# Scoring the HGRN2 levels in two column halves, with a score tile ordered by chunk half

## The chip, the cores and the metric

The kernel runs on one core of a Trainium2 chip. The metric is device time in microseconds for one execution of the whole layer (2048 tokens, width 1024, F32 inputs and outputs). Below, PE is TensorE's matmul unit and PEld its weight load, DVE is VectorE, ACT is ScalarE, POOL is GpSimd and SP is SyncE.

## The reference

The reference is one decoder layer: two head groups side by side (a gated linear recurrence, HGRN2, with 4 heads of width 128, and a sliding-window attention with sinks), an output projection, a gated MLP with a causal convolution, and a final norm. The change concerns the recurrence only. In each chunk of 64 tokens the reference computes, for each head,

```
b      = cumsum(log_f)                       # per key channel
scores = einsum('bhtk,bhsk,bhtsk->bhts', q, k, exp(b_t - b_s)),  s <= t
intra  = einsum('bhts,bhsv->bhtv', scores, v)
inter  = einsum('bhtk,bhkv->bhtv', q * exp(b), state)
out    = intra + inter
state  = state * exp(b_last) + einsum('bhsk,bhsv->bhkv', k * exp(b_last - b), v)
```

with k = 1 - f. The decay between a query t and a key s differs by channel, so the scores are not one plain matmul.

## The kernel before, in words

The sequence is worked in two halves of 1024 tokens (`for hf in range(NH)`, L1103). Each half has a mixing stage (recurrence and attention, 42 to 372 us and about 1100 to 1437 us of the span) and an MLP stage. In the mixing stage the generators `hgrn` (one for each head) and `attend` (one for each pair of query heads) are advanced in the order written out in ORDER (L40): `f`, `q`, `l`, `s` and `p` are the five steps of a recurrence head, `qa`, `sc`, `pv` and `pw` those of attention. Within that order a scheduler at build time interleaves the instructions of the steps on each engine; matmuls of a later step fill the places where an earlier one would wait. The large projections run as three matmuls in a reduced F32 form with 512 (L218) or 256 (L630 to L632) moving columns; the small matmuls of the recurrence and of the attention output (L446) run in full F32, which leaves two records for each matmul in the profile.

Step `l` computes the scores of all chunks. The kernel uses chunks of 128 tokens (TT = 8 of them in a half) and splits the decay by levels m = 1, 2, 4, ..., 64. At level m the tokens fall into blocks of 2m; keys of the first m and queries of the last m of a block meet, and their decay is the product of what each has gathered up to the border between them. K and Q are multiplied by these factors as the levels go on (L523 and L524, or L534 and L535). The tokens of the second four chunks of a half lie in reversed order within groups of 32, so "first" and "last" change places there.

The tile ST holds the scores of a head: partitions are keys, then chunk, then 128 queries.

- L481: GpSimd clears keys 64 to 127 against queries 0 to 63. L486 computes the diagonal, 64 keys by 64 queries in each matmul, 16 matmuls; L489 writes it to ST through the identity.
- Levels 1 to 16 (L512 to L524, L540 to L545): ScalarE gathers into G the keys of chunk u and of chunk u + 4 that are keys at this level (L515). One matmul for each of four u multiplies 128 such keys by 128 queries (64 of each chunk) into a PSUM tile of 512 columns (L517). Only blocks that belong together are wanted; VectorE copies them into ST under a mask (L542).
- Level 32 (32 columns of weights, 32 moving) and level 64 (64 columns of weights, 64 moving, in the two column halves of the array in turn): L531, copied to ST by ScalarE (L548, L552).

Step `s` transposes K (L564), forms the state updates (L571) and chains the states in SS (L575, L578). Step `p` adds, for each chunk, scores times values and queries times state into PSUM (L590, L592), squares the result on ScalarE for the norm (L593), scales it and transposes it. The eight chunks of a half take two PSUM tiles of four chunks each, `po`.

Of the kernel before, what the change touches and what calls it, by code (L numbers as in the profile page):

```python
# [8 lines left out]
F32 = mybir.dt.float32  # L9
# [3 lines left out]
AF = mybir.ActivationFunctionType  # L13
# [4 lines left out]
P = 128  # L18
# [5 lines left out]
TT = HALF // P  # L24
# [25 lines left out]
def hymba_layer(ctx: ExitStack, tc: tile.TileContext, a: dict, out: bass.AP, rows_out: bass.AP):  # L50
    nc = tc.nc
# [275 lines left out]
        v = t.rearrange("p (g r) -> p g r", r=32)  # L327
        return v[:, :, ::-1] if turn else v

    def across(t, base, dims):  # L330

        v = t[:, :]
        return bass.AP(v.tensor, v.offset + base, [list(v.ap[0])] + dims)

    def rows(kv):
        return slice(kv * HD, (kv + 1) * HD)
# [123 lines left out]
    def hgrn(hf, h, X, invb, vs, WG, gates, mix, p, fu=None):  # L460
# [16 lines left out]
        nc.vector.tensor_tensor(Q, q, f, op=ALU.mult)  # L477


        ST = p.tile([P, TT, P], F32, tag="t4", name="ST", bufs=2)  # L480
        nc.gpsimd.memset(ST[rows(1), :, 0:64], 0.0)  # L481
        pd = ps("hg", "pdiag")
        for c in range(TT):
            for k in range(2):
# [1 line left out]
                nc.tensor.matmul(pd[rows(k), c * 64:(c + 1) * 64], K[:, ts], q[:, ts], start=True, stop=True)  # L486
        for k in range(2):
            r = rows(k)
            nc.vector.tensor_tensor(ST[r, :, r], pd[r].rearrange("p (c t) -> p c t", t=64),  # L489
                                    ident[r, r].unsqueeze(1).to_broadcast([64, TT, 64]), op=ALU.mult)  # L490


# [15 lines left out]
        for m in LEVELS:  # L508
            nb = HALF // (2 * m)
            pl = ps("hg", "plev")  # L510
            if m < 32:
                n, nu = 64 // m, TT // 2  # L512
                far, near = [[512 - m, 2], [P, nu], [2 * m, n], [1, m]], [[512 + m, 2], [P, nu], [2 * m, n], [1, m]]
                G = p.tile([P, 512], F32, tag="G", name="G", bufs=2)
                nc.scalar.copy(across(G, 0, [[m, 2], [P, nu], [2 * m, n], [1, m]]), across(K, 0, near))  # L515
                for u in range(nu):
                    marks[m] = nc.tensor.matmul(across(pl, u * 64, [[256, 2], [1, 64]]), G[:, u * P:(u + 1) * P],  # L517
                                                across(Q, u * P + m, [far[0]] + far[2:]), start=True, stop=True)
                nf = P // m
                Kv, Qv = across(K, 0, near), across(Q, m, far)  # L520
                Fk = across(F, 1, [[4 * nf - 1, 2], [nf, nu], [2, n], [0, m]])
                Fq = across(F, 0, [[4 * nf + 1, 2], [nf, nu], [2, n], [0, m]])
                nc.vector.tensor_tensor(Kv, Kv, Fk, op=ALU.mult)  # L523
                nc.vector.tensor_tensor(Qv, Qv, Fq, op=ALU.mult)  # L524
            else:
                Qv = Q.rearrange("p (b w m) -> p b w m", w=2, m=m)
                Kv = K.rearrange("p (b w m) -> p b w m", w=2, m=m)
                for c in range(TT):
                    for s0 in range(0, P, 2 * m):
                        o = pl[s0:s0 + m, c * m:(c + 1) * m] if m < 64 else pl[rows(c % 2), c // 2 * m:(c // 2 + 1) * m]  # L530
                        nc.tensor.matmul(o, K[:, c * P + s0:c * P + s0 + m],  # L531
                                         Q[:, c * P + s0 + m:c * P + s0 + 2 * m], start=True, stop=True)
                Fv = F.rearrange("p (b w) -> p b w", w=2)
                nc.vector.tensor_tensor(Qv[:, :, 1], Qv[:, :, 1], Fv[:, :, 0:1].to_broadcast([P, nb, m]), op=ALU.mult)  # L534
                nc.vector.tensor_tensor(Kv[:, :, 0], Kv[:, :, 0], Fv[:, :, 1:2].to_broadcast([P, nb, m]), op=ALU.mult)  # L535
# [3 lines left out]
            F = Fn  # L539
            if m < 32:  # L540
                mk = C.lmask[m].bitcast(U32).rearrange("p s t -> p (s t)")
                nc.vector.copy_predicated(across(ST.rearrange("p c t -> p (c t)"), m, far),  # L542
                                          across(mk, 0, [[64, 2], [0, nu], [m, n], [1, m]]),
                                          pl.rearrange("p (s u b m) -> p s u b m", s=2, u=nu, m=m))
                continue  # L545
            if m == 64:
                for k in range(2):
                    nc.scalar.copy(ST[0:m].rearrange("p (c k) t -> p c k t", k=2)[:, :, k, m:],  # L548
                                   pl[rows(k), 0:TT // 2 * m].rearrange("p (c m) -> p c m", m=m))
                continue  # L550
            for s0 in range(0, P, 2 * m):
                nc.scalar.copy(ST[s0:s0 + m, :, s0 + m:s0 + 2 * m],  # L552
                               pl[s0:s0 + m, 0:TT * m].rearrange("p (c m) -> p c m", c=TT))
        yield
        v = vs[h]
# [26 lines left out]
        on = p.tile([P, TT, P], F32, tag="t4", name="on", bufs=2)  # L582
        ss = p.tile([P, TT], F32, tag="ss", name="ss", bufs=2)
        po = [ps("hg", "po") for _ in range(NB)]
        for c in range(TT):
            cs = slice(c * P, (c + 1) * P)
            prev = state[:, h] if c == 0 else SS[:, c - 1]
            o = po[c // 4][:, c % 4 * P:(c % 4 + 1) * P]
            empty = hf == 0 and c == 0
            marks["po"] = nc.tensor.matmul(o, ST[:, c], v[:, c], start=True, stop=empty)  # L590
            if not empty:
                marks["po"] = nc.tensor.matmul(o, Q[:, cs], prev, start=False, stop=True)  # L592
            nc.scalar.activation(on[:, c], o, AF.Square, accum_out=ss[:, c:c + 1])  # L593
        rs = rsqrt(ss, TT, 1.0 / P)
        if h == HG - 1:
            mix[h] = new_x()
# [605 lines left out]
```

## Time and profile before

| what | us |
|---|---|
| median of 3 runs | 2149.85 (2149.7 to 2150.18) |
| span of the profiled execution | 2149.0 |
| the profiled execution's own time beside it | not listed apart from the three runs; they lie 0.7 to 1.2 above the span |
| PE busy | 2130.8 |
| DVE busy | 1632.2 |
| ACT busy | 1020.2 |
| first mixing stage (42 to 372): PE, DVE, ACT busy | 328.6, 228.7, 163.0 |
| second mixing stage (1100 to 1437): PE, DVE, ACT busy | 335.6, 229.9, 165.3 |

A row of a timeline reads: start in us from the start of the span, time from the first start to the last end, engine, line, operation, output<-input, rows by columns of the weights, moving operand, how many of the same follow each other, and in brackets idle time of the engine before it with what ended it. Matmuls overlap, and the end of one is modelled; so the price of a group is read from start to start of what stands around it. A group of one line (in the views by line) gives minimum, median and maximum duration in ns, first and last start, and the shapes.

### The profile page before, as it was taken

The numbers are of one execution on the slowest core, as the hardware profiler recorded it, in microseconds if no ns is written. First come the engines' busy times: TensorE is split into PE (matmuls) and PEld (weight loads), VectorE is DVE, ScalarE is ACT, GpSimd is POOL, SyncE is SP. The second block draws the span as 40 slices with busy tenths as digits, with TensorE's granted clock in tenths as the row PEclk, the third lists the DMA queues.
The fourth block names the chain that finished last, engine by engine and source line by source line (L and its number), as shares of the span: only waits on it lengthen the run. The fifth ranks groups of instructions, "written<-read, shape, count | busy, mean of one in ns | idle before, by whom it ended". The sixth has DMA issues, their size and how long they took to land.

```text
span 2149.0 us, 29228 instructions
## 1 busy us (share of the span) xinstructions
PE 2130.8 (99%) x11271; PEld 1790.6 (83%) x11271; DVE 1632.2 (76%) x2443; ACT 1020.2 (47%) x1818; POOL 16.2 (1%) x45
## 2 busy tenths in 40 slices
PE   8999999999999999999999999999999999999998
PEld 6988988888888888888889889888888888888887
DVE  6576768788887888785775767677988888787765
ACT  5445554564444445345634446535544444443453
POOL 2000000000000000000000000000000000000000
PEclk9999999999999999999999999999999999999999
DMA  4111012413332334974641111124223323359743
GB/s 158 40 30 40 31 30 79 137 62 125 94 122 89 103 118 147 371 255 145 217 138 40 30 31 33 40 75 158 69 104 103 118 84 122 95 187 398 236 147 133
DMA packets 91147, 254.41 MB, mean 118 GB/s; under 512 B 11136, under 2 KB 13952, under 8 KB 91008
## 3 DMA queue, kind: packets, MB, share of 16 engines
q1 hardware_dynamic: 90576, 252.29, 35.3%
q8 instruction: 88, 1.44, 0.3%
q14 instruction: 51, 0.42, 0.1%
q10 hardware_dynamic: 432, 0.27, 0.0%
HBM read 195.37 MB, written 57.15 MB: 118 GB/s over the span
## 4 chain that ended last, share of the span: by engine, by line
PE 93%; DVE 5%; ACT 1%; issue 1%; DMA 0%; SPq 0%; DVEq 0%; ACTq 0%
PE X L767 7%; PE X L766 7%; PE X L765 7%; PE pop L218 6%; PE q L218 4%; PE f L218 4%; PE hq L218 4%; PE Y L767 4%; PE Y L765 4%; PE Y L766 4%; PE pdx L954 3%; PE pdx L953 3%; PE pdx L952 3%; PE g L218 3%; PE pdy L953 3%; PE pdy L954 3%
## 5 line engine op out<-in xcount | busy, mean ns | idle before, releaser
L638 ACT CAST whi<-raw 128x1024 fp32r<-128x1024 f32 x88 | 92.7, 1053 | 115.5 <-PE X L766 71.1
L765 PE MATMUL X<-T,whi 128*128 128x512 f32 x352 | 136.9, 389 | 0.0
L766 PE MATMUL X<-T,whi 128*128 128x512 f32 x352 | 136.9, 389 | 0.0
L767 PE MATMUL X<-T,wlo 128*128 128x512 f32 x352 | 136.9, 389 | 0.0
L836 DVE SCALAR_TENSOR_TENSOR y<-ga,cw,y 128x1024 f32<-128x1024 f32 x88 | 112.7, 1280 | 25.9 <-ACT y L834 25.8
L639 DVE TENSOR_TENSOR wlo<-raw,whi 128x1024 fp32r<-128x1024 f32 x88 | 107.3, 1219 | 4.4 <-ACT whi L638 4.4
L771 ACT COPY u<-X 128x512 f32<-128x512 f32 x88 | 51.6, 586 | 122.5 <-PE X L767 122.2
L199 ACT CAST whi<-raw 128x1024 fp32r<-128x1024 f32 x58 | 60.5, 1048 | 98.8 <-issue 20.6
L639 DVE TENSOR_TENSOR xld<-raw,xhd 128x1024 fp32r<-128x1024 f32 x72 | 81.1, 1132 | 17.8 <-ACT xhd L638 17.6
L638 ACT CAST xhd<-raw 128x1024 fp32r<-128x1024 f32 x72 | 69.8, 978 | 39.1 <-DMA raw<-act0T 14.0
L218 PE MATMUL pop<-XL,whi 128*128 128x512 f32 x256 | 84.2, 392 | 0.9 <-DVE XL L230 0.9
L218 PE MATMUL pop<-XH,wlo 128*128 128x512 f32 x256 | 83.3, 391 | 0.8 <-DVE wlo L200 0.8
L218 PE MATMUL pop<-XH,whi 128*128 128x512 f32 x256 | 83.1, 396 | 0.8 <-ACT XH L229 0.5
L200 DVE TENSOR_TENSOR wlo<-raw,whi 128x1024 fp32r<-128x1024 f32 x58 | 70.5, 1220 | 9.8 <-ACT whi L199 9.8
L767 PEld LDWEIGHTS X<-T,wlo 128*128 128x128 f32 x352 | 66.1, 188 | 13.7
L766 PEld LDWEIGHTS X<-T,whi 128*128 128x128 f32 x352 | 66.1, 188 | 13.7
L765 PEld LDWEIGHTS X<-T,whi 128*128 128x128 f32 x352 | 66.0, 188 | 13.7
L630 PE MATMUL pvv<-whi,XH 128*128 128x256 f32 x256 | 73.0, 286 | 0.0
L631 PE MATMUL pvv<-whi,XL 128*128 128x256 f32 x256 | 72.9, 286 | 0.0
L632 PE MATMUL pvv<-wlo,XH 128*128 128x256 f32 x256 | 71.9, 285 | 0.0
L767 PE MATMUL X<-B,wlo 128*128 128x512 f32 x176 | 68.7, 390 | 0.7 <-DVE wlo L639 0.7
L765 PE MATMUL X<-T,Sh 128*128 128x512 f32 x176 | 68.7, 390 | 0.0
(390 smaller groups left out, 6399.2 us busy)
## 6 DMA issues: line engine op xcount, KB each, us to landing
wr<-in_w_down SPq DMA_DIRECT2D x90, 512.0 KB, 5.6
raw<-in_w_gate SPq DMA_DIRECT2D x44, 512.0 KB, 3.6
raw<-in_w_up SPq DMA_DIRECT2D x44, 512.0 KB, 3.6
raw<-act0T SPq DMA_DIRECT2D x20, 512.0 KB, 5.9
raw<-act1T SPq DMA_DIRECT2D x20, 512.0 KB, 5.6
act0B<-y SPq DMA_DIRECT2D x33, 256.0 KB, 2.3
act1B<-y SPq DMA_DIRECT2D x33, 256.0 KB, 2.4
raw<-in_w_out SPq DMA_DIRECT2D x16, 512.0 KB, 3.7
```

The source lines that it names most:

```text
L218: nc.tensor.matmul(o[b], w, x[:, bs], start=f, stop=l)
L630: nc.tensor.matmul(o[:, 0:256], xh[:, t], hi[:, c], start=kt == 0, stop=False)
L631: nc.tensor.matmul(o[:, 0:256], xl[:, t], hi[:, c], start=False, stop=False)
L632: nc.tensor.matmul(o[:, 0:256], xh[:, t], lo[:, c], start=False, stop=kt == KT - 1)
L638: nc.scalar.copy(h, src)
L639: return (eng or nc.vector).tensor_tensor(l, src, h.bitcast(F32), op=ALU.subtract)
L765: nc.tensor.matmul(o, wh[:, ws], xh, start=i == 0 and not more, stop=False, skip_group_check=more)
L766: nc.tensor.matmul(o, wh[:, ws], xl, start=False, stop=False, skip_group_check=more)
L767: nc.tensor.matmul(o, wl[:, ws], xh, start=False, stop=i == 3, skip_group_check=more)
L836: nc.vector.scalar_tensor_tensor(y, g[:, w:w + HALF], C.cw[:, ft, w:w + 1], y, op0=ALU.mult, op1=ALU.add)
L953: nc.tensor.matmul(o, wh[:, i, c], al[:, i, cols], start=False, stop=False, skip_group_check=more)
L954: nc.tensor.matmul(o, wl[:, i, c], ah[:, i, cols], start=False, stop=l, skip_group_check=more)
```

## The change

The matmul of levels 1 to 16 becomes two, one for each half of a 128-column piece of G: 64 keys by the 64 queries that can belong to them. The half k writes PSUM partitions 64k to 64k + 63, so 256 columns of the PSUM tile are used in place of 512. The masked copy becomes two as well, one for each half of the partitions. ST is ordered by chunk half: partition, then half of the queries (64 each), then chunk, then query. The diagonal, the copies of levels 32 and 64 and the clearing follow the new order. In step `p` the matmul of scores and values becomes two, one for each half of a chunk's queries, which write the two halves of the PSUM partitions; for each PSUM tile all eight of them come first, then the four matmuls of queries and state, each followed by its square.

```
-    def across(t, base, dims):
+    def across(t, base, dims, r=slice(0, P)):
-        v = t[:, :]
+        v = t[r, :]
...
-        ST = p.tile([P, TT, P], F32, tag="t4", name="ST", bufs=2)
-        nc.gpsimd.memset(ST[rows(1), :, 0:64], 0.0)
+        ST = p.tile([P, 2, TT, 64], F32, tag="t4", name="ST", bufs=2)
+        nc.gpsimd.memset(ST[rows(1), 0], 0.0)
...
-            nc.vector.tensor_tensor(ST[r, :, r], pd[r].rearrange("p (c t) -> p c t", t=64),
+            nc.vector.tensor_tensor(ST[r, k], pd[r].rearrange("p (c t) -> p c t", t=64),
...
+                half = [[2 * m, n // 2], [1, m]]
                 for u in range(nu):
-                    marks[m] = nc.tensor.matmul(across(pl, u * 64, [[256, 2], [1, 64]]), G[:, u * P:(u + 1) * P],
-                                                across(Q, u * P + m, [far[0]] + far[2:]), start=True, stop=True)
+                    for k in range(2):
+                        t0 = u * P + k * 64
+                        marks[m] = nc.tensor.matmul(across(pl, u * 32, [[P, 2], [1, 32]], rows(k)), G[:, t0:t0 + 64],
+                                                    across(Q, t0 + m, [far[0]] + half), start=True, stop=True)
...
-                nc.vector.copy_predicated(across(ST.rearrange("p c t -> p (c t)"), m, far),
-                                          across(mk, 0, [[64, 2], [0, nu], [m, n], [1, m]]),
-                                          pl.rearrange("p (s u b m) -> p s u b m", s=2, u=nu, m=m))
+                for k in range(2):
+                    nc.vector.copy_predicated(
+                        across(ST.rearrange("p k c t -> p (k c t)"), k * 512 + m, [[256 - m, 2], [64, nu]] + half, rows(k)),
+                        across(mk, k * 32, [[64, 2], [0, nu], [m, n // 2], [1, m]], rows(k)),
+                        pl[rows(k), 0:256].rearrange("p (s u b m) -> p s u b m", s=2, u=nu, m=m))
...
-                    nc.scalar.copy(ST[0:m].rearrange("p (c k) t -> p c k t", k=2)[:, :, k, m:],
+                    nc.scalar.copy(ST[0:m, 1].rearrange("p (c k) t -> p c k t", k=2)[:, :, k],
...
-                nc.scalar.copy(ST[s0:s0 + m, :, s0 + m:s0 + 2 * m],
+                nc.scalar.copy(ST[s0:s0 + m, s0 // 64, :, m:],
...
-        for c in range(TT):
-            cs = slice(c * P, (c + 1) * P)
-            prev = state[:, h] if c == 0 else SS[:, c - 1]
-            o = po[c // 4][:, c % 4 * P:(c % 4 + 1) * P]
-            empty = hf == 0 and c == 0
-            marks["po"] = nc.tensor.matmul(o, ST[:, c], v[:, c], start=True, stop=empty)
-            if not empty:
-                marks["po"] = nc.tensor.matmul(o, Q[:, cs], prev, start=False, stop=True)
-            nc.scalar.activation(on[:, c], o, AF.Square, accum_out=ss[:, c:c + 1])
+        for b in range(NB):
+            at = [po[b][:, i * P:(i + 1) * P] for i in range(4)]
+            empty = hf == 0 and b == 0
+            for i in range(4):
+                for k in range(2):
+                    marks["po"] = nc.tensor.matmul(at[i][rows(k)], ST[:, k, 4 * b + i], v[:, 4 * b + i],
+                                                   start=i == 0, stop=empty and i == 0, skip_group_check=True)
+            for i in range(4):
+                c = 4 * b + i
+                if not (empty and i == 0):
+                    marks["po"] = nc.tensor.matmul(at[i], Q[:, c * P:(c + 1) * P], SS[:, c - 1] if c else state[:, h],
+                                                   start=False, stop=True, skip_group_check=True)
+                nc.scalar.activation(on[:, c], at[i], AF.Square, accum_out=ss[:, c:c + 1])
```

## The prediction

> **What bounds the kernel now.** I read the page first: shares of busy time, then the chain that ended last.
>
> ```profile
> span 2149.0 us, 29228 instructions
> ```
> ```profile
> PE 2130.8 (99%) x11271; PEld 1790.6 (83%) x11271; DVE 1632.2 (76%) x2443; ACT 1020.2 (47%) x1818; POOL 16.2 (1%) x45
> ```
> ```profile
> PE 93%; DVE 5%; ACT 1%; issue 1%; DMA 0%; SPq 0%; DVEq 0%; ACTq 0%
> ```
>
> TensorE is busy all the time and carries 93% of the chain. The span is 2149.0 us and the median of the runs 2149.85, so 0.85 us lie around the span; I keep that constant. The busy time of PE is no price list, since matmuls overlap: what counts is the distance from one start to the next. So I went to the timeline of PE and read prices there. The change touches only the two mixing stages; this is the first (start:end, its length, then busy us of PE, PEld, DVE, ACT, POOL), with its last 36 us in the second row:
>
> ```profile
> 42.00:372.00 330.00, 328.59 (x2367) 287.57 (x2366) 228.74 (x430) 163.02 (x429) 1.57 (x3) 1.00 0.14 42
> 336.00:372.00 36.00, 34.64 (x277) 28.70 (x276) 27.14 (x49) 13.04 (x46) 0.00 (x0) 1.00 0.22 73
> ```
>
> PE idles 1.4 us of 330 (330.00 - 328.59), nearly all of it in the last 36 (36.00 - 34.64). A microsecond of PE work that goes there is a microsecond of time, as long as nothing else steps in.
>
> **The levels.** An F32 matmul leaves two records:
>
> ```profile
> L517 PE MATMUL plev<-Q,G x320: 270/275/382, 62.3 to 1415.5; 128*128 128x128 f32 x160
> ```
>
> That is 160 matmuls: 2 halves of the sequence, 4 heads, 5 levels, 4 each; so 40 level groups of 8 records. The change makes each matmul two, on 64 keys and 64 queries: 16 records per group. Level 64 already has exactly that shape (64 columns of weights, 64 moving, the two column halves in turn), so the trace has the new price. First a group of before in the stream of 256-wide matmuls:
>
> ```profile
> 73.50 0.28 PE L631 MATMUL pvv<-whi,XL 128*128 128x256 f32 x1
> 73.62 1.06 PE L517 MATMUL plev<-Q,G 128*128 128x128 f32 x8
> 74.43 0.36 PE L632 MATMUL pvv<-wlo,XH 128*128 128x256 f32 x1
> 74.63 0.28 PE L630 MATMUL pvv<-whi,XH 128*128 128x256 f32 x1
> ```
>
> Then level 64 in the same stream:
>
> ```profile
> 91.61 0.28 PE L632 MATMUL pvv<-wlo,XH 128*128 128x256 f32 x1
> 91.81 0.69 PE L531 MATMUL plev<-Q,K 128*64 128x64 f32 x16
> 92.43 0.39 PE L630 MATMUL pvv<-whi,XH 128*128 128x256 f32 x1
> 92.65 0.28 PE L631 MATMUL pvv<-whi,XL 128*128 128x256 f32 x1
> 92.77 0.28 PE L632 MATMUL pvv<-wlo,XH 128*128 128x256 f32 x1
> ```
>
> A 256-wide matmul takes 0.12 us of the stream (92.65 to 92.77). The old group takes 74.63 - 73.50 - 2 x 0.12 = 0.89; the new shape 92.65 - 91.61 - 0.24 = 0.80. So a group that stands alone gains only 0.09 us. The 16 small records themselves are quick, but going from full-width weights to 64 columns costs 0.08 (0.20 instead of 0.12 before 91.81), and coming back costs a tail before 92.43 and 0.10 after it.
>
> A group that stands beside other 64-column work saves that passage. The first level of each head (8 groups) follows the diagonal scores, which are 64 x 64 already:
>
> ```profile
> 61.23 1.15 PE L486 MATMUL pdiag<-hg,K 128*64 128x64 f32 x32
> 62.31 1.18 PE L517 MATMUL plev<-Q,G 128*128 128x128 f32 x8
> 63.24 0.72 PE L218 MATMUL q<-XL,whi 128*128 128x512 f32 x2
> ```
>
> 32 records take 1.08 to the next start, 16 took 0.62 (91.81 to 92.43): 0.46 for 16 more. The old group took 62.31 to 63.24, 0.93. Gain 0.47 each.
>
> Six groups stand beside the 64-column matmuls of the attention output; the first and the last of them, each with its neighbour:
>
> ```profile
> 159.75 1.05 PE L517 MATMUL plev<-Q,G 128*128 128x128 f32 x8
> 160.74 0.44 PE L446 MATMUL poT<-pp,V 128*64 128x128 f32 x4
> ```
> ```profile
> 1414.40 0.31 PE L446 MATMUL poT<-po,V 128*64 128x128 f32 x2
> 1414.64 1.16 PE L517 MATMUL plev<-Q,G 128*128 128x128 f32 x8
> ```
>
> and level 64 between such matmuls:
>
> ```profile
> 269.63 0.64 PE L531 MATMUL plev<-Q,K 128*64 128x64 f32 x16
> 270.09 0.39 PE L446 MATMUL poT<-pp,V 128*64 128x128 f32 x4
> ```
>
> 0.99 becomes 0.46 to 0.54 plus 0.08 for going in: a gain of 0.37 to 0.45; I take 0.42, as one of the six has such a neighbour on both sides. Levels in all: 8 x 0.47 + 6 x 0.42 + 26 x 0.09 = **-8.6 us**.
>
> **The outputs.** The score tile is now stored by halves, so each chunk's scores times values becomes two matmuls with 64 columns of weights and 128 moving. This is where the change pays. The nearest shape is the attention output again, here a run of 8 such rows, its first, its last and what follows:
>
> ```profile
> 282.57 0.44 PE L446 MATMUL poT<-pp,V 128*64 128x128 f32 x4
> 282.84 0.39 PE L446 MATMUL poT<-po,V 128*64 128x128 f32 x4
> ...
> 283.93 0.39 PE L446 MATMUL poT<-pp,V 128*64 128x128 f32 x4
> 284.15 0.39 PE L446 MATMUL poT<-po,V 128*64 128x128 f32 x4
> 284.47 0.50 PE L218 MATMUL f<-XL,whi 128*128 128x512 f32 x1
> 284.80 0.62 PE L218 MATMUL f<-XH,wlo 128*128 128x512 f32 x2
> 285.26 0.62 PE L218 MATMUL f<-XH,whi 128*128 128x512 f32 x2
> ```
>
> and the old form:
>
> ```profile
> 115.40 0.39 PE L590 MATMUL po<-v,ST 128*128 128x128 f32 x2
> 115.62 0.28 PE L592 MATMUL po<-SS,Q 128*128 128x128 f32 x1
> ```
>
> Before, one chunk is 2 records, 0.22 us. After, it is 4 records, and 4 of them also take 0.22 (283.93 to 284.15). The halving gains nothing here, and the passage is new. The change groups four chunks, so 16 blocks: each pays 0.08 going in, 0.05 at its first row (282.57 to 282.84 is 0.27), 0.10 at its end (284.15 to 284.47 is 0.32) and 0.10 on the next matmul (0.33 to 284.80, against 0.46 for the two after it): 0.33. Four heads' outputs already follow attention outputs, the first and last of these:
>
> ```profile
> 208.59 0.39 PE L446 MATMUL poT<-po,V 128*64 128x128 f32 x4
> 208.91 0.71 PE L590 MATMUL po<-v,ST 128*128 128x128 f32 x4
> ```
> ```profile
> 1431.25 0.49 PE L590 MATMUL po<-v,ST 128*128 128x128 f32 x2
> ```
>
> There the passage is paid today (0.32 from 208.59 to 208.91) and only moves: 0. So 12 x 0.33 = **+4.0 us**; bounds 2.6 (one block per head, both banks together) and 5.3 (all 16 alone).
>
> **VectorE, ScalarE, GpSimd.** Each masked copy into the score tile becomes two, on 64 partitions and half the columns:
>
> ```profile
> L542 DVE COPY_PREDICATED ST<-lmask,plev x40: 693/726/1341, 65.2 to 1416.6; 128x512 f32<-128x512 uint32 x40
> ```
> ```profile
> L408 DVE COPY_PREDICATED sc<-own,psc x64: 391/443/508, 100.7 to 1403.9; 128x256 f32<-128x256 uint32 x64
> ```
>
> 2 x 0.44 against 0.73: 0.16 more, 40 times, some 6.5 us on an engine with 228.7 of 330 busy. It is hidden by PE's own work, which doesn't wait for the score tile until much later. The cover is gone where the last head's levels run out of other work:
>
> ```profile
> 349.51 0.68 PE L517 MATMUL plev<-Q,G 128*128 128x128 f32 x4 [0.44 <-DVE Q L524]
> ```
>
> Queued behind a masked copy there are the next level's K and Q products. Three copies at the end of each mixing stage, 0.16 each, twice: at most 0.9, and four of the six gains beside attention outputs (1.6 us) lie in these stretches and could turn into waiting. Bounds 0 and +2.5. I take **+0.3**, nearer to 0: the level's own matmuls also end 0.1 to 0.4 sooner, which hands the K and Q products back about what the copies take. The other score copies and GpSimd's memset move as many elements as before and stay off PE's path; no DMA is added or moved, and no new wait stands on any queue.
>
> **Sum.** -8.6 + 4.0 + 0.3 = -4.3 us: span 2144.7, time **2145.5**. A difference under 0.2% (4.3 us, below 2145.55 or above 2154.15) is about what a measurement can't tell from none, so the forecast stands on the edge.
>
> **Rivals.**
> *The outputs fall apart (slower).* If the order puts each chunk's two halves on their own, next to its Q matmul as today, there are 64 small blocks in place of 16, each paying 0.33: 60 of them (four moved passages taken off) cost 19.8; 19.8 - 8.6 + 0.3 = +11.5, or 2161.4. At (8.6 - 0.3) / 0.33 = 25 paying blocks the change is even, at 38 (4.3 / 0.33 = 13 more) it is slower by over 0.2%. For it: L590 stands apart by chunk in the trace (115.40 between two Q matmuls). Against: the change issues all eight halves of a bank ahead of the first Q matmul and the first read. 0.10.
>
> *The order is made anew and neighbours are lost.* If the first level no longer follows the diagonal, 8 x 0.38 = 3.0 are lost; the six others 6 x 0.33 = 2.0; the ends of the stages 2.2. One or two of these give 2147.5 to 2151: no change. Against: the diagonal precedes level 1 because both wait for K, q and Q only. 0.10.
>
> *Strided queries stream slowly.* At levels 1 and 2 the moving queries have gaps. If 64 columns took twice as long, 16 groups lose 0.46 each: 2152.9. Against: 270 to 275 ns for nearly all 160 wide ones, whatever the stride. 0.04. [...]
>
> *The passages vanish or merge.* If going to 64 columns and back cost nothing, each group would go from 0.89 to 0.46 and the outputs stay even: -17.2 us, 2132.6. Against: the 0.08 and 0.10 stand in the rows. Both banks' blocks merged in each head give 2145.5 - (4.0 - 2.6) = 2144.1, five more level groups beside 64-column work (0.33 each) 2142.4. 0.10 together. [...]
>
> **How the numbers follow.** The forecast case, an order like today's, has 0.66; its own range is 2143 to 2148, a little over half of it (0.36) under 2145.55. Faster: 0.36 + 0.10 = 0.46. Within 0.2%: 0.30 + 0.10 + 0.04 = 0.44. Slower: 0.10. The range 2141 to 2151 takes in the bounds of the outputs and of the stage ends, the merged order and most of the lost neighbours; left out are the outputs that fall apart, slow strides and free passages.
>
> **What would show it.** Right: 64-column groups of 16 records at each level from 2 on, with 0.08 before and 0.10 after; 48 records in a row at the diagonal and level 1; 16 blocks of 16 records for the outputs, 0.22 per four. PE busy in the two mixing stages some 2 us shorter each, the rest of the span unchanged. Wrong: output blocks of 4 records, PE waits for L523, L524 or the masked copy outside the last 36 us of a stage, or a pair of halves that takes clearly more than 0.06 us.

## The result and the profile after

The changed kernel takes 2162.26 us in the median of four runs (2161.58 to 2162.68), the kernel before 2149.86 (2149.70 to 2150.18): ratio 1.0057, 95% interval 1.0042 to 1.0071. It is 12.4 us slower. The forecast was 2145.5, and the range (2141 to 2151) does not hold it. Line numbers from here on are those of the kernel that ran: the level matmul L517 of before is L520 after, the masked copy L542 is L546, the products L523 and L524 are L526 and L527, L590 and L592 are L595 and L600.

The page of the profile after, its span, busy times and chain:

```profile
span 2159.9 us, 30159 instructions
...
PE 2130.2 (99%) x11719; PEld 1777.6 (82%) x11719; DVE 1643.5 (76%) x2483; ACT 1018.3 (47%) x1818; POOL 16.7 (1%) x45
...
PE 91%; DVE 6%; ACT 1%; issue 1%; DMA 1%; SPq 0%; DVEq 0%; ACTq 0%
```

TensorE is 0.6 us less busy than before (2130.8) in a span that is 10.9 longer. The time went mainly into idle, not into matmuls. (The median grows by 12.4 and the profiled span by 10.9. In the runs that list both, the time lies 1.7 us above the span, here 2161.58 and 2159.9, and not 0.85 as the prediction kept; so the profiled execution of before took some 2150.7, an estimate.) The windows of the same kernel, the first mixing stage and its last 36 us:

```profile
42.00:372.00 330.00, 323.47 (x2569) 277.49 (x2567) 234.10 (x450) 160.06 (x415) 1.56 (x3) 0.99 0.14 43
336.00:372.00 36.00, 31.50 (x296) 25.55 (x295) 30.88 (x56) 10.51 (x32) 0.00 (x0) 0.95 0.24 80
```

PE idles 6.5 us of 330 (before 1.4), 4.5 of them in the last 36; VectorE has 30.9 us of work there (before 27.1). The clock in the second row is 0.95, before 1.00.

The streams themselves came out as the prediction had them. PE's timeline after, a level group between 256-wide matmuls, then an output block of four chunks:

```profile
73.82 0.28 PE L640 MATMUL pvv<-whi,XL 128*128 128x256 f32 x1
74.03 0.69 PE L520 MATMUL plev<-Q,G 128*64 128x64 f32 x16
74.65 0.39 PE L641 MATMUL pvv<-wlo,XH 128*128 128x256 f32 x1
74.87 0.28 PE L639 MATMUL pvv<-whi,XH 128*128 128x256 f32 x1
...
1179.82 0.61 PE L218 MATMUL f<-XH,wlo 128*128 128x512 f32 x2
1180.36 1.09 PE L595 MATMUL po<-v,ST 128*64 128x128 f32 x16
1181.38 0.49 PE L600 MATMUL po<-state,Q 128*128 128x128 f32 x2
```

The level group costs 74.87 - 73.82 - 2 x 0.12 = 0.81 (forecast 0.80). The output block pays 0.08 going in (0.54 in place of 0.46) and takes 1.02 for 16 records, where the forecast's prices give 4 x 0.22 + 0.05 + 0.10 = 1.03.

So the waits carry most of the loss. The largest waits of PE in the whole run after (sum in us, times, longest), but for the one of 6.4 us for the first input, which before has too (6.2):

```profile
PE pop L218 <- ACT G L515: 3.6, 2, 1.8
PE q L218 <- ACT whi L199: 2.3, 2, 1.2
PE pop L218 <- DVE XL L230: 1.9, 2, 1.0
PE q L218 <- DVE wlo L200: 1.6, 2, 0.8
PE plev L534 <- DVE Q L527: 1.6, 2, 0.8
PE ppt L435 <- DVE sc L408: 1.3, 2, 0.7
```

All six stand in the mixing stages, each once per half. Two of them name ScalarE and lead back to VectorE. The first names the wrong engine: L515 ended by chance at about the same time. What PE waits for is VectorE's L500, which empties the PSUM tile of the gate: this matmul starts 0.15 us after the end of the first L500 in the changed kernel, and as long after it in e2, e9 and e12 below. VectorE's timeline of before shows where L500 stood:

```profile
338.76 0.51 DVE L408 COPY_PREDICATED sc<-own,psc 128x256 f32<-128x256 uint32 x1
339.16 1.28 DVE L500 TENSOR_TENSOR hg<-g,invb 128x512 f32<-128x512 f32 x2
340.35 1.22 DVE L200 TENSOR_TENSOR wlo<-raw,whi 128x1024 fp32r<-128x1024 f32 x1
341.48 0.69 DVE L438 TENSOR_TENSOR po<-ppt,ownT 128x512 f32<-128x512 f32 x1
```

and the same stretch after:

```profile
339.36 1.50 DVE L546 COPY_PREDICATED ST<-lmask,plev 64x256 f32<-64x256 uint32 x2
340.89 0.44 DVE L408 COPY_PREDICATED sc<-own,psc 128x256 f32<-128x256 uint32 x1
341.23 0.68 DVE L438 TENSOR_TENSOR po<-ppt,ownT 128x512 f32<-128x512 f32 x1
341.83 0.68 DVE L438 TENSOR_TENSOR pp<-ppt,prevT 128x512 f32<-128x512 f32 x1
342.43 0.68 DVE L526 TENSOR_TENSOR K<-K,F 128x512 f32<-128x512 f32 x1
343.02 1.28 DVE L500 TENSOR_TENSOR hg<-g,invb 128x512 f32<-128x512 f32 x2
```

L500 starts 3.9 us later. VectorE is already 2.2 us later at L230, a few rows earlier (335.33 before, 337.51 after, not shown); then the masked copies take longer, and two L438 and one product stand ahead of L500. There is no gap on VectorE in either. PE's timeline after shows the price, which has two parts:

```profile
343.85 0.77 PE L218 MATMUL pop<-XH,whi 128*128 128x512 f32 x1 [1.81 <-ACT G L515]
344.42 0.63 PE L218 MATMUL pop<-XL,whi 128*128 128x512 f32 x1
344.84 0.63 PE L218 MATMUL pop<-XH,whi 128*128 128x512 f32 x1
345.27 0.63 PE L218 MATMUL pop<-XL,whi 128*128 128x512 f32 x1
```

After the wait the matmuls come every 0.43 us in place of 0.23 (two in 0.46, as in the rows of the prediction), for about 3 us: the granted clock is halved there. The windows of the kernel after, the 3.4 us up to the fall of the clock and the 3.4 us behind it (the third number from the end of a row is the granted clock):

```profile
340.36:343.78 3.42, 1.00 (x16) 0.63 (x12) 3.39 (x7) 0.62 (x1) 0.00 (x0) 1.00 0.39 140
343.78:347.19 3.41, 3.34 (x8) 2.57 (x9) 3.41 (x5) 1.17 (x2) 0.00 (x0) 0.50 0.21 49
```

The second of the two stands at 257 us (q on ScalarE's cast, L199). Here ScalarE is late itself, and VectorE is behind it: the cast follows the softmax's exponentials, and these wait for VectorE's L416 and L417 (ScalarE idles 2.44 us up to 251.97 for L416), which stand behind a masked copy of the levels in VectorE's queue.

The sums over PE's whole timeline, from each start to the next, idle apart: idle 5.4 to 17.9 us (+12.5), level matmuls -11.2, diagonal -0.8, attention outputs -1.0, outputs' two lines +2.6, the other small matmuls that now stand next to 64-column work +3.8 (L639 to L641, L399, L435), and L218 +5.8, some 3 of it the half clock. Without the idle that is 0.6 us less, where the forecast had 4.6 less (-8.6 + 4.0); the half clock is most of the difference. The start and the end of the span are 1.0 shorter.

### The profile page after: what moved, and what is told of

Read it like the earlier page. It is cut to its first block, busy times and chain, and to the rows that moved or that the text cites. A ratio compares the mean times of both kernels' runs of the same rounds, so it can differ in the third digit from the quotient of the medians.

```text
span 2159.9 us, 30159 instructions
## 1 busy us (share of the span) xinstructions
PE 2130.2 (99%) x11719; PEld 1777.6 (82%) x11719; DVE 1643.5 (76%) x2483; ACT 1018.3 (47%) x1818; POOL 16.7 (1%) x45
## 4 chain that ended last, share of the span: by engine, by line
PE 91%; DVE 6%; ACT 1%; issue 1%; DMA 1%; SPq 0%; DVEq 0%; ACTq 0%
PE X L776 7%; PE X L775 7%; PE X L774 7%; PE pop L218 6%; PE hq L218 4%; PE q L218 4%; PE f L218 4%; PE Y L775 4%; PE Y L776 4%; PE Y L774 4%; PE g L218 3%; PE pdx L961 3%; PE pdx L963 3%; PE pdx L962 3%; PE pdy L961 3%; PE pdy L962 3%
## 5 line engine op out<-in xcount | busy, mean ns | idle before, releaser
L199 ACT CAST whi<-raw 128x1024 fp32r<-128x1024 f32 x58 | 60.3, 1048 | 86.7 <-issue 23.7
L218 PE MATMUL pop<-XH,whi 128*128 128x512 f32 x256 | 84.5, 402 | 3.8 <-ACT G L515 3.6
L218 PE MATMUL pop<-XL,whi 128*128 128x512 f32 x256 | 85.0, 396 | 1.9 <-DVE XL L230 1.9
L218 PE MATMUL pop<-XH,wlo 128*128 128x512 f32 x256 | 84.4, 396 | 1.2 <-DVE wlo L200 1.2
L200 DVE TENSOR_TENSOR wlo<-raw,whi 128x1024 fp32r<-128x1024 f32 x58 | 70.4, 1219 | 10.1 <-ACT whi L199 10.1
L639 PE MATMUL pvv<-whi,XH 128*128 128x256 f32 x256 | 73.1, 287 | 0.0
L641 PE MATMUL pvv<-wlo,XH 128*128 128x256 f32 x256 | 72.3, 287 | 0.0
```

The source lines that it names most:

```text
L218: nc.tensor.matmul(o[b], w, x[:, bs], start=f, stop=l)
L639: nc.tensor.matmul(o[:, 0:256], xh[:, t], hi[:, c], start=kt == 0, stop=False)
L641: nc.tensor.matmul(o[:, 0:256], xh[:, t], lo[:, c], start=False, stop=kt == KT - 1)
```

## The experiments

Two theories at the start. **V**: VectorE's longer queue is the price. **G**: TensorE's gain is given back where it comes earlier than casts and softmax, in an order laid out anew. That the order is new is a fact: with neighbouring rows of one kind counted once, at least 107 of VectorE's 2141 rows of before and 254 of PE's 6711 no longer stand in the old order after (some of PE's are the regrouped outputs themselves). Times are medians; the difference is to the kernel before on the same chip.

| run | us | difference | ratio, 95% |
|---|---|---|---|
| e1 copies alone, 128x256 | 2150.30 | +0.5 | 1.0002 [0.9992, 1.0011] |
| e10 copies alone, 64x256 | 2155.04 | +4.9 | 1.0023 [1.0014, 1.0032] |
| e2 levels, copies 64x256 | 2152.07 | +2.2 | 1.0010 [1.0000, 1.0019] |
| e16 levels, copies 128x256 | 2145.28 | -4.7 | 0.9979 [0.9969, 0.9988] |
| e5 levels, one copy 128x256 | 2147.27 | -2.8 | 0.9987 [0.9978, 0.9997] |
| e3 outputs, copies 64x256 | 2160.63 | +10.8 | 1.0052 [1.0035, 1.0069] |
| e17 outputs, copies 128x256 | 2156.81 | +6.8 | 1.0030 [1.0019, 1.0042] |
| e4 outputs, one copy 128x256 | 2157.11 | +7.0 | 1.0034 [1.0022, 1.0047] |
| the change | 2162.26 | +12.4 | 1.0057 [1.0042, 1.0071] |
| e9 the change, copies 128x256 | 2155.32 | +5.2 | 1.0024 [1.0015, 1.0034] |
| e6 the change, one copy 128x256 | 2148.79 | -1.0 | 0.9995 [0.9986, 1.0005] |
| e11 as e9, outputs chunk by chunk | 2173.75 | +23.6 | 1.0111 [1.0096, 1.0126] |
| e12 as e9, gate first | 2157.17 | +7.2 | 1.0033 [1.0021, 1.0045] |
| e13 the change, gate first | 2164.38 | +14.4 | 1.0067 [1.0053, 1.0080] |
| e14 as e9, scale on ScalarE | 2156.24 | +6.2 | 1.0030 [1.0020, 1.0041] |
| e15 before, scale on ScalarE | 2152.23 | +2.2 | 1.0010 [1.0001, 1.0019] |
| e7 the change, low parts on GpSimd | 2170.48 | +20.4 | 1.0099 [1.0084, 1.0114] |
| e8 before, low parts on GpSimd | 2166.32 | +16.2 | 1.0075 [1.0060, 1.0090] |
| e18 levels, old tile and outputs | 2146.15 | -3.9 | 0.9982 [0.9973, 0.9991] |

### One part at a time: e1, e2, e3, e6

e1 is the kernel before with its masked copy in two pieces, by the four first and the four second chunks:

```
-nc.vector.copy_predicated(across(ST..., m, far), across(mk, 0, [[64, 2], ...]), pl...)
+for s in range(2):
+    nc.vector.copy_predicated(across(ST..., m + s * (512 - m), far[1:]), across(mk, s * 64, ...),
+                              pl[:, s * 256:(s + 1) * 256]...)
```

> The kernel before, with each masked copy of levels 1 to 16 as two copies of 128 x 256 (one for each four chunks): the VectorE work of the change (about 0.16 us more for each of 40 levels) with nothing else of it. Theory V (VectorE binds the ends of the mixing stages, and its longer queue there is what the change pays): slower by 4 to 12 us, 2154 to 2162, with TensorE waits of the new size at the stage ends. Theory G (TensorE's gain is given back where weight casts and softmax are only just in time, and the instructions are laid out anew; VectorE's 0.16 us are hidden): within 1 to 2 us of 2149.9.

Measured +0.5. It looked as if V had fallen. It had not been tried, as e9 and e10 show below: 80 copies of 0.44 us came in place of 40 of 0.73, but from start to start they took 33.7 us of VectorE's queue in place of 32.4.

e2 is the changed kernel with the outputs of before, on 128 neighbouring columns of the new tile:

```
+nc.tensor.matmul(o, ST.rearrange("p k c t -> p (k c t)")[:, cs], v[:, c], start=True, stop=empty)
```

> The changed kernel with the outputs as before (one matmul with 128 columns of weights for each chunk; it reads 128 neighbouring columns of the new score tile, so scores of other chunks enter). Level matmuls and split copies alone. Stream price: 4.0 us less TensorE work than the changed kernel. Theory V: the waits stay, about 2158. Theory G: the gain of the levels is partly given back, 2146 to 2152.

e3 is the changed kernel with the level matmuls of before (128 keys by 128 queries):

```
+marks[m] = nc.tensor.matmul(across(pl, u * 64, [[256, 2], [1, 64]]), G[:, u * P:(u + 1) * P], ...)
```

> The changed kernel with the level matmuls as before (128 keys by 128 queries); split copies, new score tile and the grouped outputs stay. 8.6 us more TensorE work in the levels than the changed kernel. Theory V: that work fits in the waits, so 2160 to 2165. Theory G: no gain to give back, only the price of the outputs, 2154 or a little more.

e6 is the changed kernel with one masked copy per level over all 128 partitions into one half of the tile:

```
-for k in range(2):
-    nc.vector.copy_predicated(across(ST..., k * 512 + m, ...), across(mk, k * 32, ..., rows(k)), pl[rows(k), 0:256]...)
+nc.vector.copy_predicated(across(ST..., m, ...), across(mk, 0, ...), pl[:, 0:256]...)
```

> The changed kernel with one masked copy of 128 x 256 for each level in place of two of 64 x 256 (the keys 64 to 127 land in the wrong half of the score tile): VectorE has 0.44 us for a level where the changed kernel has 0.88 and the kernel before 0.73. Theory V: the waits at the stage ends go and the time falls below the kernel before, 2138 to 2147. Theory G: the waits for weight casts stay, 2155 to 2162.

The levels alone lose 2.2 us, the outputs alone 10.8; taking one copy of two away wins 13.4 on the change. So the copies seem to matter after all. By the forecasts e2 stands next to G's, e3 in V's, and e6 between the two. Each of these kernels has an order of its own, though, so they don't separate V from G.

### Fewer copies, and work moved to GpSimd: e4, e5, e7, e8

e4 and e5 are e3 and e2 with the one copy of e6.

> Leaves out: the masked copy of one half of the keys lands in the wrong place, and half of the scores of levels 1 to 16 are not copied. The grouped outputs with the wide level matmuls, and one masked copy of 128x256 per level in place of two of 64x256 (VectorE 22 us in copies in place of 44). V, VectorE's longer queue is the price: the 5.4 us of new waits of the outputs alone go, 2153 to 2155, which is the stream price of the outputs (3 to 4 us) over the kernel before. G, the laying out anew that the outputs cause is the price, whatever VectorE has to do: 2158 to 2161.

> Leaves out: as the levels alone, the outputs read 128 neighbouring columns of the new tile, and the masked copy of one half of the keys lands in the wrong place. Narrow level matmuls, outputs as before, one masked copy of 128x256. V: the 11 us of stream that the levels save show nearly in full, 2139 to 2143. G: most of it is given back where TensorE arrives before the casts and the softmax, 2146 to 2150.

Measured +7.0 and -2.8: e4 (2157.1) lies between the two forecasts, e5 (2147.3) in G's. The levels' gain stays small even with half the copying.

e7 and e8 move line 230 in the changed kernel and in the kernel before:

```
-M[n] = split(mix[n])
+M[n] = split(mix[n], eng=nc.gpsimd)
```

> The changed kernel with the low parts of the mixed inputs (1.21 us each on VectorE, line 230) made on GpSimd, with an order of TensorE that is almost the changed kernel's own. It takes more off VectorE at the ends of the mixing stages than the masked copies add. V: the waits for VectorE there go, 2148 to 2153, unless GpSimd is so late that the projections wait for it instead. G: the waits stay, since they come from the order and from ScalarE's casts, 2159 to 2163.

> The same move in the kernel before, as the control. V and G alike: TensorE waits there for VectorE 2 to 3 us in all, so 2147 to 2150.5; if GpSimd is late, above 2151, and then the run of the changed kernel with the same move says little.

Both lose. GpSimd takes 2.8 to 3.0 us on average (e7) for what VectorE does in 1.22. PE's longest new wait, 3.42 us, is not for GpSimd, though: it is for a gather (L515) that follows VectorE's K product, and that product is slow while GpSimd works. Timelines of GpSimd and of VectorE in e7:

```profile
332.12 6.18 POOL L230 TENSOR_TENSOR XL<-att,XH 128x1024 fp32r<-128x1024 f32 x2
```
```profile
333.18 2.88 DVE L526 TENSOR_TENSOR K<-K,F 128x512 f32<-128x512 f32 x1
```

The eight K and Q products that run beside L230 on GpSimd take 2.44 us in the median, the others 0.69. The control loses 16.2 us, so e7 says nothing of the change.

### The copies at an unchanged order: e10 and e9

In these traces a duration is not the time for which an instruction holds its engine. VectorE's timeline of before, one level and what follows it:

```profile
249.61 0.71 DVE L542 COPY_PREDICATED ST<-lmask,plev 128x512 f32<-128x512 uint32 x1
250.21 0.68 DVE L523 TENSOR_TENSOR K<-K,F 128x512 f32<-128x512 f32 x1
```

after:

```profile
249.41 0.87 DVE L546 COPY_PREDICATED ST<-lmask,plev 64x256 f32<-64x256 uint32 x2
250.31 0.69 DVE L526 TENSOR_TENSOR K<-K,F 128x512 f32<-128x512 f32 x1
```

and e9, whose copies run over all partitions:

```profile
248.56 0.76 DVE L546 COPY_PREDICATED ST<-lmask,plev 128x256 f32<-128x256 uint32 x2
249.22 0.68 DVE L526 TENSOR_TENSOR K<-K,F 128x512 f32<-128x512 f32 x1
```

Before, the next product starts 0.60 us after a copy of 0.71, that is 0.11 before its end. After, the pair takes 0.90: each copy is over before the next instruction starts. In e9 the pair takes 0.66. Over all levels (medians from start to start, 24 groups of levels 4 to 16 and 16 of levels 1 and 2): before 0.61 and 1.11, after 0.93 and 1.53, e9 and e1 0.66 and 1.11. In sum (24 times the one and 16 times the other) 32.4 us before, 46.7 after, 33.7 in e9 and e1.

The copies of e9 differ from the changed kernel's in the number of partitions and in that all start at partition 0. L388 tells the two apart: it works on 64 partitions, in turn from 0 and from 64, and the next row shown starts at 0. VectorE's timeline of before has both:

```profile
240.93 0.67 DVE L388 TENSOR_TENSOR ql<-att,qh 64x512 fp32r<-64x512 f32 x1
241.53 0.43 DVE L408 COPY_PREDICATED sc<-own,psc 128x256 f32<-128x256 uint32 x1
...
246.67 0.69 DVE L388 TENSOR_TENSOR ql<-att,qh 64x512 fp32r<-64x512 f32 x1
247.38 0.45 DVE L408 COPY_PREDICATED sc<-own,psc 128x256 f32<-128x256 uint32 x1
```

The first is left 0.07 us before its end, the second 0.02 after it. So it is in both mixing stages of before, among the L388 with no wait behind them: of seven from 0 whose next row starts at 0 as well, six are left 0.07 to 0.08 us before their end and one 0.03 after it; all six from 64 are left 0.02 to 0.03 after it, with as many partitions. So in these rows the loss goes with a change of the first partition, not with the number of partitions; why is not shown. For the masked copies it is 0.93 us a pair with the change of partition (levels 4 to 16, the changed kernel) against 0.66 without (e9).

e10 is the kernel before with copies of the changed kernel's size and rows, e9 the changed kernel without `rows(k)` in the three operands (the mask of a level is zero for the keys of the other half, so all 128 partitions can be named):

```
-across(ST..., k * 512 + m, [...] + half, rows(k)), across(mk, k * 32, [...], rows(k)), pl[rows(k), 0:256]...
+across(ST..., k * 512 + m, [...] + half),          across(mk, k * 32, [...]),          pl[:, 0:256]...
```

> Leaves out: half of the scores of levels 1 to 16 are not copied and some land in the wrong place. The kernel before with its masked copies in the size of the changed kernel, two of 64x256 per level; the matmuls stay. The copies alone as tried first were 128x256, which overlap their neighbours and so made VectorE's queue only 1.3 us longer; these make it 14.5 us longer. V: 2154 to 2160, with waits of TensorE at the ends of the mixing stages. G: 2149 to 2151.

> The changed kernel, but each of the two masked copies of a level runs over all 128 partitions (the mask is zero for the keys of the other half), 128x256 in place of 64x256. In the traces a copy on 64 partitions holds VectorE until 0.03 us after its end, one on 128 partitions lets the next instruction start 0.10 us (levels 4 to 16) or 0.21 us (levels 1 and 2) before its end: 24 pairs at 0.94 and 16 at 1.53 us would become 24 at 0.66 and 16 at 1.11, 13 us less of VectorE's queue with as many instructions. V, VectorE's longer queue is the price: 2148 to 2153. G, the new order and the gain given back are the price, however long the copies hold VectorE: 2158 to 2163.

Measured +4.9 for e10, in V's range, and 7.2 less than the change for e9, between the two forecasts. The order is no part of either: against the changed kernel, e9 has no row out of its place on PE, VectorE or ScalarE; e10 and e1 have one and the same order on PE, 13 rows of which no longer stand as before, and differ by one row each on VectorE and ScalarE. So V is shown, for some 4.4 to 4.9 us by itself (against e1 and against before) and 7.2 in the change. G is not refuted: e9 stays 5.2 over before.

### Looking for the other 5 us: e11 to e15

e11 issues two halves, the matmul of queries and state and the square for each chunk by itself.

> As e9 (the copies over all partitions), and the outputs chunk by chunk: two halves, then the matmul of queries and state, then the square. If TensorE then takes each chunk by itself, 64 passages to 64 columns in place of 13 to 16, at 0.2 to 0.33 us each: 10 to 16 us more than e9. If the scheduler keeps neighbouring chunks together, within 3 us of e9. If the grouping by four is itself the price (four squares that wait for one bank), 2 to 5 us less than e9.

PE's timeline in e11:

```profile
119.69 0.44 PE L596 MATMUL po<-v,ST 128*64 128x128 f32 x4
120.06 0.49 PE L598 MATMUL po<-SS,Q 128*128 128x128 f32 x2
120.47 0.44 PE L596 MATMUL po<-v,ST 128*64 128x128 f32 x4
120.84 0.49 PE L598 MATMUL po<-SS,Q 128*128 128x128 f32 x2
```

The outputs do fall apart: 62 runs of them, nearly all of 4 records, 0.78 us for each chunk with its query matmul. It costs 18.4 us more than e9, over the 10 to 16 expected. The grouping by four is worth that much, and is not itself a price.

e12 moves the gate in e9's written order, e13 in the changed kernel's:

```
-"... m5 sc3 g2 pv3 pw3 m2 g3 s3 p3"
+"... m5 sc3 g2 g3 pv3 pw3 m2 s3 p3"
```

> As e9, and in the written order g3, the last head's gate, stands ahead of pv3 in place of behind pw3. That puts the two products which free the gate's PSUM tile (line 500) ahead of two products of the attention (line 438) on VectorE at the end of each mixing stage, and changes little else; in the kernel before the same edit changes no place in any engine's order. O, the order laid out anew is the other half of the price: in e9 TensorE still waits 1.7 us for line 500 in each stage and then runs at half clock for about 3 us, so 3 us of waits and 3 us of slow clock go: 2148 to 2151. Without O (VectorE's length alone): 2154.5 to 2156.5, as e9.

> The changed kernel with its own 64-row copies and with g3 ahead of pv3 in the written order. O and V as two separate prices: 2155 to 2158, that is the 5 to 7 us of O off and the 7 us of V (e9) still on. If the one wait only gives way to the next while VectorE's queue is this long: 2160 to 2163.

Neither is faster, and both lie above all the ranges expected. They read 2 us slower, but the intervals overlap with those of e9 and of the change. VectorE's timeline in e12, and the row of PE there:

```profile
337.44 1.29 DVE L500 TENSOR_TENSOR hg<-g,invb 128x512 f32<-128x512 f32 x2
...
339.23 0.70 DVE L438 TENSOR_TENSOR po<-ppt,ownT 128x512 f32<-128x512 f32 x1
...
340.43 1.24 DVE L200 TENSOR_TENSOR wlo<-raw,whi 128x1024 fp32r<-128x1024 f32 x1
```
```profile
341.72 0.73 PE L218 MATMUL pop<-XH,wlo 128*128 128x512 f32 x2 [2.21 <-DVE wlo L200]
```

L500 stands ahead of both L438 now, as wanted, and its wait is gone. PE now waits 2.21 us for the next thing in VectorE's queue, the low part of the next weights. L200 starts at 340.43 here and at 340.35 in the kernel before: PE is earlier, VectorE is not. So the place of this one instruction is not the price.

e14 and e15 take the scaling of the softmax (19.6 us in all) off VectorE, in e9 and in the kernel before:

```
-nc.vector.tensor_tensor(sc, sc, den.unsqueeze(3).to_broadcast([P, 2, 4, P]), op=ALU.mult)
+for kv in range(2):
+    for i in range(4):
+        nc.scalar.activation(sc[:, kv, i], sc[:, kv, i], AF.Identity, scale=den[:, kv, i:i + 1])
```

> As e9, and the scaling of the softmax (line 426, 16 times 1.22 us on VectorE) as eight products of 128 columns on ScalarE. If the 5 us that e9 keeps over the kernel before are waits for a VectorE that is full at the ends of the mixing stages, taking 2.4 us of it away in each should win most of them: 2147 to 2152. If they are the outputs' own price or ScalarE's, 2154 or more.

> The control: the kernel before with the scaling of the softmax on ScalarE. TensorE waits there 2 to 3 us for VectorE in all, so 2147 to 2151; if it gains as much as e14 gains on e9, e14 says nothing of the change.

e14 gains nothing on e9 (+0.9), and the control loses 2.2. e14 is thus in its second range, and the control lies above its own. Both have a new order again, and eight products on ScalarE where VectorE had one. So e14 does not show what the load on VectorE is worth by itself; taking 20 us off it was no gain here.

### Adding up: e16, e17 and a version that keeps the gain, e18

e16 and e17 are e2 and e3 with the copies of e9; on PE, VectorE and ScalarE their order is that of e2 and e3.

> Leaves out: as the levels alone, the outputs read 128 neighbouring columns of the new tile. The levels alone (e2) in the same order on every engine, with the masked copies over all partitions, so that VectorE has about as much to do as in the kernel before. If the copies on 64 rows were all that ate the 8.6 us of the levels: 2141 to 2143. If the ends of the mixing stages have a length of their own, a chain over VectorE, so that TensorE only waits longer there: 2146 to 2150.

> The outputs alone (e3) in the same order on every engine, with the masked copies over all partitions. If the outputs cost their stream alone: 2153 to 2155. If the order laid out anew costs waits at the stage ends even with cheap copies: 2156 to 2159. e16 and e17 together with e9 tell whether the two parts add up: e9 is 5.2 us over the kernel before.

The levels win 4.7 us, between the two ranges expected; the outputs cost 6.8, in the range for waits. Together they would make +2.1; e9 has +5.2, so 3.1 come from their meeting. And at an unchanged order the copies that start at partition 64 cost, in turn: 4.4 (e10 - e1), 6.9 (e2 - e16), 4.0 (e3 - e17), 7.2 (the change - e9).

e18 keeps the narrow level matmuls and puts everything else back. The one masked copy of before reads each PSUM column twice, for both halves of a chunk's queries, under the mask:

```
+to = [[512 - m, 2], [P, nu], [64, 2]] + half
+nc.vector.copy_predicated(across(ST.rearrange("p c t -> p (c t)"), m, to),
+                          across(mk, 0, [[64, 2], [0, nu], [32, 2], [m, n // 2], [1, m]]),
+                          across(pl, 0, [[P, 2], [32, nu], [0, 2], [m, n // 2], [1, m]]))
```

> A whole version with the gain and without the two prices: the levels in two column halves as in the change, but the score tile and the outputs as before, and one masked copy of 128x512 per level that reads each PSUM column twice, for both halves of a chunk's queries, under the mask. VectorE then has what it has before and TensorE has the levels' gain alone, as in e16: 2144 to 2147. If the order, which is laid out anew once more, costs waits as in e9: 2148 to 2152.

2146.15 us (2145.34 to 2146.91), ratio 0.9982, 0.9973 to 0.9991: it beats both kernels. Its copies, and its first mixing stage:

```profile
L546 DVE COPY_PREDICATED ST<-lmask,plev x40: 698/726/1350, 64.9 to 1410.7; 128x512 f32<-128x512 uint32 x40
```
```profile
42.00:372.00 330.00, 327.72 (x2536) 281.91 (x2536) 230.36 (x444) 162.40 (x429) 1.57 (x3) 1.00 0.14 43
```

The copies are those of before again, 40 of 0.73 us; PE idles 2.3 us and the clock is whole.

Where the time lies, in us between marks on PE's timeline: from the diagonal of head 0 to that of head 3 (middle), and from there to the first matmul of the MLP (end), for both mixing stages, each row from one profiled execution:

| | middle 1 | end 1 | middle 2 | end 2 |
|---|---|---|---|---|
| before | 259.3 | 121.2 | 259.4 | 121.5 |
| e10 (copies) | +0.8 | +2.1 | 0.0 | +2.1 |
| e16 (levels) | -3.0 | +0.9 | -2.9 | +1.8 |
| e17 (outputs) | +2.0 | +1.4 | +3.5 | +0.4 |
| e9 (both) | +0.1 | +2.1 | +0.7 | +2.6 |
| the change | +1.6 | +2.8 | +2.2 | +3.9 |
| e18 | -3.0 | +0.7 | -3.0 | +0.2 |

The levels win in the middles only. None of these wins at an end, though each end holds a whole head's levels. In the second end of e16, 3.41 us run at half clock (1402.27 to 1405.68), which is up to 1.7 us of its +1.8; e18 has no such stretch and wins nothing at the ends either.

## Why the prediction was wrong

**The levels (-8.6).** The price of a group was right (0.81 measured, 0.80 forecast), and so was what stands beside what: 48 records in a row at the diagonal and level 1. In e18 the streams are 7.3 us shorter (level matmuls -11.2, diagonal -0.8, against +4.7 on what follows them). PE's idle rises by 2.1, so 5.2 arrive between the two profiled executions; in the medians 3.9 arrive for e18 and 4.7 for e16. The share that lies at the ends was taken as gained, since PE hardly idles there; PE got its work done sooner and waited.

**The outputs (+4.0).** The count was right: apart from one block that other work enters, they run in 16s and 32s. In e17 the streams are 4.8 us longer and idle is 2.0 more, 6.8 in time. The idle is a term that the prediction did not have.

**VectorE and the stage ends (+0.3): the step that failed.** "2 x 0.44 against 0.73: 0.16 more, 40 times, some 6.5 us" took durations for the time that VectorE is held. From start to start it is some 14 us (46.7 - 32.4). A row of before had it: the two L489 on 64 partitions. VectorE's timeline there:

```profile
322.15 1.38 DVE L489 TENSOR_TENSOR ST<-pdiag,ident 64x512 f32<-64x512 f32 x2
323.56 0.69 DVE L523 TENSOR_TENSOR K<-K,f 128x512 f32<-128x512 f32 x1
```

Two of them take 1.41, while the two L500 on 128 partitions, as long each, take 1.19 (339.16 to 340.35). And "it is hidden by PE's own work, which doesn't wait for the score tile until much later" was the wrong cover. Nobody waits for the score tile, but other things wait behind the copy in VectorE's queue: the gate's product, the low parts of weights, the maximum of the softmax. That is also why its own signs of being wrong did not show it: it named waits for L523, L524 or the copy outside the last 36 us, and the waits there name the casts and low parts of weights (1.16 and 0.81 us, 257 and 262 us). The prediction looked at the last 36 us, with 27.1 us of VectorE. The window 16 us earlier, in before, shows that there was no room:

```profile
320.00:356.00 36.00, 34.89 (x254) 28.93 (x253) 35.63 (x54) 18.64 (x42) 0.00 (x0) 1.00 0.38 115
```

35.63 of 36 us. Its bound of +2.5 was too low for the same reason; the term measures 4.0 to 7.2.

**The sum.** By parts at equal copies: -4.7 (levels, e16) + 6.8 (outputs, e17) + 3.1 (their meeting) + 7.2 (copies) = 12.4.

**The rivals.** The outputs did not fall apart; 2161.4 came near the measured time by chance. Had they done so, it would have cost 18.4 us (e11), about the 15.8 that the prediction gave (19.8 less 4.0). That the order is made anew was a rival with lost neighbours as its price. It was made anew, the neighbours stayed, and the price was waiting: idle +12.5 us after. No rival had VectorE as the bound of the stage ends, and that was the one to have.

**What stays open.** The 3.1 us of the meeting, and why the waits at the ends stay with cheap copies. Part of the 3.1 may be the clock: the profiled execution of e9 has two stretches of 3.41 us at half clock, that of e16 one, that of e17 none, and each loses at most 1.7 us (half of 3.41, an estimate). How much of it stands in the medians isn't shown, since these executions of e9 and e16 were 1.6 and 1.3 us above theirs. As to the waits, taking one away calls up the next (e12), and 20 us less on VectorE did not help (e14). e6 has the same two parts with one copy and is 6.2 us faster than e9, while e4 and e5 gain nothing from the same saving (+0.2 and +1.9 against e17 and e16). All these differ in order. That an order laid out anew is worth a few us by itself is likely, but not shown: e12 and e13 alone have the same work in another order (10 of PE's rows and 15 of VectorE's out of place), and their 2 us are not clear of the noise.

## What to carry to other kernels

Price an instruction by the distance to the next start, on VectorE as on TensorE, and look for a row that changes the first partition: splitting one copy over all partitions into two halves of the partitions cost here twice what the durations say (14 us in place of 6.5). Before work is called hidden, look at the queue that it stands in, in the stretch where that engine is fullest, and ask who waits for what stands behind it. When a change has a part that pays and a part that makes it possible, look for an access pattern that gives the first without the second (e18).

## What else the runs showed

After a wait of 1.81 us in the changed kernel, and from 1.2 us after the end of one of 2.21 in e12, matmuls of 512 columns came every 0.43 us in place of 0.23 for a stretch of 3.41 us (granted clock 0.50 from 343.78 to 347.19 us of the changed kernel), some 1.5 us lost on top of the wait. The wait of 1.81 us thus cost nearly twice its length. The length of one wait does not tell when: after 1.21 in e2 the clock fell too, while after 1.16 at 257 us of the changed kernel it stayed at 1.00. Nor does PE's idle time in the 3.41 us before, a window as long as the slow stretch: where the clock fell it was 2.4 us in the changed kernel (a wait of 0.68 stands ahead of the 1.81), 2.2 in e12, 1.8 in e2 and 1.5 in e16; where the clock stayed whole it was 1.2 up to 257 us of the changed kernel and 1.7 in e3. What makes the clock fall isn't shown.

The masked copy of levels 1 and 2, which writes single values or pairs with gaps, took nearly twice the time of levels 4 to 16 for as many elements (1.11 against 0.61 us from start to start in the kernel before). And work moved to GpSimd was not free for VectorE: its products with two inputs took 2.44 us beside GpSimd's in place of 0.69 (e7).
